# One decoder layer on one core: the two parts of the recurrence's and the branch's weights made by transfers instead of by VectorE

## The chip, the core and the metric

The kernel runs on one core of one Trainium2 chip. A core has a matrix engine (TensorE, PE in the profile; PEld is its loading of stationary operands), VectorE (DVE), ScalarE (ACT), GpSimd (POOL) and SyncE (SP), each with an instruction queue of its own that it executes in order. Transfers between HBM and the on-chip memory SBUF are issued by an engine (here SP or POOL) and then run on 16 DMA engines. Products are accumulated in the banks of PSUM. The metric is the device time of one execution in microseconds, and smaller is better.

## The reference, cut to what matters

One layer for a sequence of 512 tokens with 1024 channels: a SwiGLU feed-forward block, a mixer with two branches (dilated attention, and a gated recurrence), and a second feed-forward block, each between two RMS norms. The part that the change touches:

```python
u = rms_norm(h, mix_norm_pre[l])
proj = u @ w_in[l]                                   # 1024 x 8704
q, k, v, xr, yr, gl = jnp.split(proj, splits, axis=-1)
...
rec = rg_lru_branch(xr, conv_w[l], ...) * jax.nn.gelu(yr)
rec_d = rec @ w_rec_branch[l]                        # 1024 x 1024
gates = jax.nn.sigmoid(gl).reshape(B, S, N_BRANCHES, D_MODEL)
merged = gates[:, :, 0] * attn_d + gates[:, :, 1] * rec_d
h = h + rms_norm(merged @ w_out[l], mix_norm_post[l])
```

`rg_lru_branch` is a causal convolution of width 4, two gates made by small products (`lru_w_x`, `lru_w_a`, 256 x 256 for each of 4 heads) with a sigmoid, and a linear recurrence over the tokens. Everything is float32.

## The kernel before

Channels lie on the 128 partitions and tokens along the free dimension. A product of 1024 by 512 channels and tokens is done in tiles: one weight tile of 128 output channels holds 8 blocks of 128 x 128, for 8 blocks of input channels.

To keep float32 accuracy, each operand is split into a high part in the rounded format fp32r and a low part, also fp32r, that holds the rest. `mm3` (L263 to L266) makes three matmuls of a block: high by high (L264), high weight by low activation (L265), low weight by high activation (L266). `gemm` runs the 8 blocks of a tile, 24 matmuls of 512 columns, into one PSUM bank of tag `acc` (5 banks) or `aux` (3 banks).

All weights stand in one stream in HBM, `wst`, in the order of use (`stream_plan`), and `stream_groups` cuts it into groups of at most 2048 columns, one load each. `raw_of` starts the load of the next group on SP's queue (L199) into one of two buffers of tag `raw`, and hands out its parts. `fetch` takes a tile from there, a buffer of tag `w8` (4 buffers for tiles over 512 columns, each with room for both parts) and makes the parts by `split`:

```python
def split(dh, dl, src):
    ACT.activation(dh, src, AF.Copy)
    DVE.tensor_sub(dl, src, dh.bitcast(F32))
```

L251 is the copy on ACT, which rounds to fp32r; L252 is the subtraction on DVE. In the groups of the profile a weight tile is `w`.

The stages around the change, in the program's order: attention and its branch product (weights ("attn", m), 512 columns, tag `w4`); then the recurrence, a loop over 4 heads; then the branch product with the weights ("rec", m); then `w_out`, and the second feed-forward block. A head of the recurrence does, in this order: two products for `xr` (keys ("in", 36 + c)), each followed by DVE's evacuation (L968), the convolution (ACT L971, DVE L973) and a split into `rec`; two products for `yr` (keys ("in", 44 + c)) with DVE's evacuation (L985) and gelu on ACT (L986); the gates' products from `rec` with the weights ("lru", head), into `aux` banks that ACT's sigmoid empties (L1001); the coefficients and the scan (ACT L1010 to L1017, DVE L1013 to L1022); and a number of products for the branch gate (keys ("in", 60 + c): 0, 2, 2, 4 of them by head) with DVE L1028 and ACT L1029. The branch product has 8 tiles, each followed by DVE (L1036, L1037) and a split. So 24 tiles "in", 4 tiles "lru" and 8 tiles "rec" pass through `w8` there, all of 1024 columns.

The order of the instructions on each engine is not the program's. It is laid out when the kernel is built, by a list scheduler with planned durations: an engine takes the ready instruction with the best priority, and the program's order gives the priority. `tc.high_priority(offset=AHEAD)` lifts the instructions of `fetch` by 100 places, evacuations by 200. Once laid out, each queue is fixed and executes in order; waits are semaphores. POOL's queue before holds only transfers of activations and of the kept residual (L677, L681, L743, L911, L1056, L1067).

Of the kernel before, what the change touches and what calls it, by code (L numbers as in the profile page):

```python
# [10 lines left out]
F32 = mybir.dt.float32  # L11
F32R = mybir.dt.float32r
AF = mybir.ActivationFunctionType
ALU = mybir.AluOpType
AX = mybir.AxisListType

P = 128
# [11 lines left out]
RAW_W = 2048  # L29
# [38 lines left out]
def stream_plan():  # L68

    plan = []  # L70

    def ffn(n):
        for ev in ffn_order():
            if ev[0] == "std":
                plan.append((("gate", n, ev[1]), 1024))
                plan.append((("up", n, ev[1]), 1024))
            elif ev[0] == "prep":
                plan.append((("gu", n, ev[1]), 2048))
            else:
                for m in ev[-1]:  # L80
                    plan.append((("down", n, ev[-2], m), down_width(ev[-2])))
        for m in range(KC):
            plan.append((("down", n, len(FF_PARTS) - 1, m), down_width(len(FF_PARTS) - 1)))

    def values(g):
        for k in range(4):
            plan.append((("v", g, k), 1024))

    def qk(h):
        for g in range(NG):  # L90
            plan.append((("pair", g * 4 + h, 12 + g * 4 + h), 2048))

    ffn(1)
    del plan[:4]
    for k in range(KC):
        plan.insert(k, (("start", k), 512))
    for g in VALUES:
        values(g)
    for h in range(NH):
        qk(h)  # L100
    for c in range(0, KC, 2):
        plan.append((("pair", 52 + c, 53 + c), 2048))
    for m in range(KC):
        plan.append((("attn", m), 512))
    for h in range(NH):
        for c in (2 * h, 2 * h + 1):
            plan.append((("in", 36 + c), 1024))
        for c in (2 * h, 2 * h + 1):
            plan.append((("in", 44 + c), 1024))
        plan.append((("lru", h), 1024))  # L110
        for c in GATE1[h]:
            plan.append((("in", 60 + c), 1024))
    for m in range(KC):
        plan.append((("rec", m), 1024))
    for m in range(KC):
        plan.append((("out", m), 1024))
    ffn(2)
    return plan


def stream_groups():

    groups, cur, w = [], [], 0
    for key, width in stream_plan():
        if w + width > RAW_W or (cur and cur[0][0][0] == "start"):
            groups.append(cur)
            cur, w = [], 0
        cur.append((key, w, width))
        w += width
    groups.append(cur)  # L130
    return groups


SMALL = {}
# [10 lines left out]
def hybrid_layer(ctx: ExitStack, tc: tile.TileContext, xT: bass.AP, wst: bass.AP, small: bass.AP,  # L145
                 consts: bass.AP, bias: bass.AP, out: bass.AP):
    nc = tc.nc
    DVE, ACT, PE = nc.vector, nc.scalar, nc.tensor
# [37 lines left out]


    groups = stream_groups()
    state = {"g": 0, "i": 0, "off": 0, "raw": None}

    def raw_of(key):

        g, i = state["g"], state["i"]
        grp = groups[g]
        if i == 0:
            w = grp[-1][1] + grp[-1][2]
            raw = wpool.tile([P, RAW_W], F32, name="raw", tag="raw", bufs=2)
            src = bass.AP(tensor=wst.tensor, offset=wst.offset + state["off"], ap=[[w, P], [1, w]])
            nc.sync.dma_start(raw[:, :w], src)  # L199
            state["raw"] = raw  # L200
            state["off"] += w * P
        k, o, w = grp[i]
        assert k == key, (k, key)
        src = state["raw"][:, o:o + w]
        if i + 1 == len(grp):
            state["g"], state["i"] = g + 1, 0
        else:
            state["i"] = i + 1
        return src

    def fetch(key, slot=None):

        with tc.high_priority(offset=AHEAD if slot is None else 0):
            src = raw_of(key)
            w = src.shape[-1]
            t = slot() if slot else w8() if w > 512 else w4()
            split(t[:, 0, :w], t[:, 1, :w], src)
            return t[:, 0, :w], t[:, 1, :w]

    def w8():  # L220
        return wpool.tile([P, 2, 1024], F32R, name="w8", tag="w8", bufs=4)

    def w4():
        return wpool.tile([P, 2, 512], F32R, name="w4", tag="w4", bufs=3)
# [25 lines left out]
# [3 lines that stand above are left out]
# [7 lines left out]
    def tmp(name):  # L260
        return tpool.tile([P, T], F32, name=name, tag="t")
# [23 lines left out]
    def gemm_first(keys, x, slots=None):  # L285

        wts = [fetch(k, None if i < 4 else slots.pop(0)) for i, k in enumerate(keys)]
        pss = [acc_ps() for _ in keys]
        for sl in HALVES:
            for k in range(x.n):  # L290
                for wt, ps in zip(wts, pss):
                    mm3(ps[:, sl], k128(wt[0])[:, k, :], k128(wt[1])[:, k, :], x.hi[k][:, sl],
                        x.lo[k][:, sl], k == 0, k == x.n - 1)
        return pss
# [61 lines left out]
    def last_product(key, x, evac, gi, nxt, then, slots, end=False):  # L356
# [6 lines left out]
        for m in range(KC - nl):  # L363
            ps = acc_ps()
            gemm(ps, fetch(key(m)), x)
            evac(m, ps, FULL)
            sq_add(acc, lambda s: facc[:, m, s], FULL, m == 0)
            ACT.activation(facc[:, m, :], facc[:, m, :], AF.Copy, scale=gain(gi, m))
        if nl < 8:
            warm(acc)  # L370
        wts = [fetch(key(m), None if m < 4 else slots.pop(0)) for m in range(KC - nl, KC)]
        for sl in HALVES:
            for m in range(KC - nl, KC):
# [285 lines left out]
    for i, nm in enumerate(("g1b", "g2b")):  # L659
        o, w = SMALL[nm]  # L660
# [25 lines left out]
    with ExitStack() as mx:  # L686
# [59 lines left out]
        t, steps = x_forms("gma", r2, apool, facc)  # L746
# [37 lines left out]
        scale = -1.0 / math.sqrt(P)  # L784
# [117 lines left out]
        for c in range(0, KC, 2):  # L902
            g, u = tmp("g"), tmp("u")
# [17 lines left out]
    with ExitStack() as mx:  # L921
        rpool = mx.enter_context(tc.tile_pool(name="rec", bufs=1))
        rec_t = rpool.tile([P, 16, T], F32R, name="rec")
        rec = Act([rec_t[:, i, :] for i in range(8)], [rec_t[:, 8 + i, :] for i in range(8)])
# [7 lines left out]
        o, w = SMALL["ap"]  # L932
# [26 lines left out]
        for hd in range(NH):  # L959
# [32 lines left out]
            for j in range(2):  # L992
                c = 2 * hd + j
                gs = []
                for w, bn in ((1, "ba"), (0, "bx")):
# [4 lines left out]
                    g = lpool.tile([P, T], F32, name="gt", tag="gt", bufs=4)  # L1000
# [172 lines left out]
```

## Time and profile before

| | |
|---|---|
| median of 3 runs | 1273.09 us (1272.76 to 1273.25) |
| profiled execution, its own time | 1272.06 us |
| its span, first to last instruction | 1270.3 us |
| busy share of the span | PE 98%, PEld 89%, DVE 77%, ACT 56%, POOL 2% |
| recurrence (24 "in" and 4 "lru" tiles) | 649 to 807 us of the span |
| branch product (8 "rec" tiles) | 807 to 851 us |
| HBM read and written | 127.07 MB and 6.29 MB |

How the lines are read: a group of instructions is given as line, engine, operation, output <- input with the count, then the busy time and the mean duration in ns, then the engine's idle time just before these instructions and what ended it. In a row of stages (from:to) the numbers behind the length are the busy time and the count of each engine in the order of its heading, then the granted clock of TensorE, the busy share of the 16 DMA engines and what they moved in GB/s. In a row of waits, "A <- B: us, times, longest" says how long A's engine stood until B was done. A row of transfers gives the count, the size, and the median time from issue to landing.

### The profile page before, as it was taken

The numbers are of one execution on the slowest core, as the hardware profiler recorded it, in microseconds if no ns is written. First come the engines' busy times: TensorE is split into PE (matmuls) and PEld (weight loads), VectorE is DVE, ScalarE is ACT, GpSimd is POOL, SyncE is SP. The second block draws the span as 40 slices with busy tenths as digits, with TensorE's granted clock in tenths as the row PEclk, the third lists the DMA queues.
The fourth block names the chain that finished last, engine by engine and source line by source line (L and its number), as shares of the span: only waits on it lengthen the run. The fifth ranks groups of instructions, "written<-read, shape, count | busy, mean of one in ns | idle before, by whom it ended". The sixth has DMA issues, their size and how long they took to land.

```text
span 1270.3 us, 19619 instructions
## 1 busy us (share of the span) xinstructions
PE 1247.0 (98%) x7952; PEld 1129.1 (89%) x7952; DVE 971.9 (77%) x1561; ACT 715.3 (56%) x1193; POOL 20.0 (2%) x42
## 2 busy tenths in 40 slices
PE   9999999999999999999999999999999999999996
PEld 7889999999887999999988777889988999999995
DVE  7987777777688788889676877753998777777755
ACT  6555444445555565556637997636555544444453
POOL 0000000000002000000100000000000000000000
PEclk9999999999999999999999999999999999999998
DMA  6222222233614322221441231323222222222342
GB/s 238 72 86 102 102 104 104 103 110 113 216 66 148 114 100 83 75 101 68 135 156 41 100 133 67 133 89 111 100 100 91 92 100 100 100 100 86 118 146 67
DMA packets 26937, 135.66 MB, mean 107 GB/s; under 512 B 3424, under 2 KB 5600, under 8 KB 14688
## 3 DMA queue, kind: packets, MB, share of 16 engines
q1 hardware_dynamic: 24192, 122.88, 27.2%
q0 software_dynamic: 2656, 11.54, 2.7%
q8 instruction: 62, 1.02, 0.3%
q14 instruction: 27, 0.22, 0.1%
HBM read 127.07 MB, written 6.29 MB: 105 GB/s over the span
## 4 chain that ended last, share of the span: by engine, by line
PE 69%; DVE 17%; ACT 7%; DMA 4%; issue 2%; SPq 0%; DVEq 0%; ACTq 0%
PE acc L509 10%; PE acc L508 10%; PE acc L510 10%; PE acc L264 9%; PE acc L266 9%; PE acc L265 9%; DVE w L252 4%; DMA raw<-in_w 4%; PE aux L508 2%; PE aux L509 2%; PE aux L510 2%; ACT w L251 2%; DVE sig L973 1%; DVE acc L316 1%; DVE h L436 1%
## 5 line engine op out<-in xcount | busy, mean ns | idle before, releaser
L251 ACT ACTIVATE w<-raw 128x1024 fp32r<-128x1024 f32 (+2 forms) x307 | 263.7, 865 | 231.4 <-PE acc L510 101.2
L252 DVE TENSOR_TENSOR w<-raw,w 128x1024 fp32r<-128x1024 f32 (+2 forms) x307 | 298.6, 986 | 83.8 <-ACT w L251 83.6
L509 PE MATMUL acc<-big,w 128*128 128x256 f32 x928 | 263.3, 284 | 0.0
L508 PE MATMUL acc<-big,w 128*128 128x256 f32 x928 | 263.1, 283 | 0.0
L510 PE MATMUL acc<-big,w 128*128 128x256 f32 x928 | 262.8, 283 | 0.0
L264 PE MATMUL acc<-act,w 128*128 128x512 f32 (+1 forms) x524 | 195.5, 374 | 3.1 <-ACT w L251 2.7
L266 PE MATMUL acc<-act,w 128*128 128x512 f32 (+1 forms) x524 | 191.9, 368 | 1.4 <-DVE w L252 1.2
L265 PE MATMUL acc<-act,w 128*128 128x512 f32 (+1 forms) x524 | 191.6, 366 | 0.0
L508 PEld LDWEIGHTS acc<-big,w 128*128 128x128 f32 x928 | 177.4, 191 | 4.0 <-ACT c L515 0.4
L510 PEld LDWEIGHTS acc<-big,w 128*128 128x128 f32 x928 | 177.7, 191 | 1.8
L509 PEld LDWEIGHTS acc<-big,w 128*128 128x128 f32 x928 | 177.5, 191 | 1.7
L264 PEld LDWEIGHTS acc<-act,w 128*128 128x128 f32 x524 | 98.7, 189 | 20.5 <-ACT w L251 6.0
L266 PEld LDWEIGHTS acc<-act,w 128*128 128x128 f32 x524 | 98.8, 189 | 18.2 <-DVE w L252 4.1
L265 PEld LDWEIGHTS acc<-act,w 128*128 128x128 f32 x524 | 98.9, 189 | 13.7
L515 ACT ACTIVATE c<-acc 128x256 f32<-128x256 f32 x166 | 62.7, 378 | 59.5 <-PE acc L510 57.7
L264 PE MATMUL acc<-big,w 128*128 128x512 f32 (+1 forms) x240 | 91.7, 382 | 0.0
L266 PE MATMUL acc<-big,w 128*128 128x512 f32 (+1 forms) x240 | 91.7, 382 | 0.0
L265 PE MATMUL acc<-big,w 128*128 128x512 f32 (+1 forms) x240 | 91.7, 382 | 0.0
L570 DVE TENSOR_TENSOR facc<-acc,facc 128x512 f32<-128x512 f32 x48 | 33.2, 692 | 57.9 <-PE acc L266 57.7
L509 PE MATMUL aux<-big,w 128*128 128x256 f32 x272 | 76.9, 283 | 0.0
L508 PE MATMUL aux<-big,w 128*128 128x256 f32 x272 | 76.9, 283 | 0.0
L510 PE MATMUL aux<-big,w 128*128 128x256 f32 x272 | 76.8, 282 | 0.0
(273 smaller groups left out, 2455.5 us busy)
## 6 DMA issues: line engine op xcount, KB each, us to landing
raw<-in_w SPq DMA_DIRECT2D x89, 1024.0 KB, 4.9
raw<-in_w SPq DMA_DIRECT2D x23, 512.0 KB, 4.8
raw<-in_w SPq DMA_DIRECT2D x6, 768.0 KB, 4.2
raw<-in_w SPq DMA_DIRECT2D x16, 256.0 KB, 4.4
raw<-in_w SPq DMA_DIRECT2D x3, 896.0 KB, 4.6
h<-in_x SPq DMA_DIRECT2D x8, 256.0 KB, 5.3
h<-in_x POOLq DMA_DIRECT2D x8, 256.0 KB, 5.4
kept_m<-h POOLq DMA_DIRECT2D x2, 1024.0 KB, 4.7
```

Of the source, the lines that this page charges most:

```text
L251: ACT.activation(dh, src, AF.Copy)
L252: DVE.tensor_sub(dl, src, dh.bitcast(F32))
L264: PE.matmul(ps, wh, xh, start=first, stop=False)
L265: PE.matmul(ps, wh, xl, start=False, stop=False)
L266: PE.matmul(ps, wl, xh, start=False, stop=last)
L316: DVE.tensor_add(acc[:, s], acc[:, s], q)
L436: DVE.scalar_tensor_tensor(o, hm(m), col(gname, m), r, op0=ALU.mult, op1=ALU.mult)
L508: PE.matmul(ps, wh, xh, start=start and k == 0, stop=False, skip_group_check=True)
L509: PE.matmul(ps, wh, xl, start=False, stop=False, skip_group_check=True)
L510: PE.matmul(ps, wl, xh, start=False, stop=k == 3, skip_group_check=True)
L515: ACT.activation(c, ps, AF.Copy)
L570: DVE.tensor_add(facc[:, m, :], ps, facc[:, m, :])
```

## The change

For the keys "in" and "rec" (32 tiles) `fetch` no longer goes through a raw buffer. Each such tile is a group of its own in the stream. A casting transfer on POOL's queue brings it from HBM into the high part, rounding on the way; ACT writes the negative of the high part into the low part; a second transfer on POOL's queue brings the same data from HBM again and adds it to the low part. The copy on ACT becomes the negative, and the subtraction on DVE is gone. The tiles "lru" and all others are made as before.

```diff
--- before.py
+++ after.py
@@ -122,13 +122,21 @@
 
     groups, cur, w = [], [], 0
     for key, width in stream_plan():
-        if w + width > RAW_W or (cur and cur[0][0][0] == "start"):
+        if cur and (w + width > RAW_W or cur[0][0][0] == "start" or in_parts(key)):
             groups.append(cur)
             cur, w = [], 0
+        if in_parts(key):
+            groups.append([(key, 0, width)])
+            continue
         cur.append((key, w, width))
         w += width
     groups.append(cur)
     return groups
+
+
+def in_parts(key):
+
+    return key[0] == "rec" or key[0] == "in"
 
 
 SMALL = {}
@@ -211,6 +219,19 @@
     def fetch(key, slot=None):
 
         with tc.high_priority(offset=AHEAD if slot is None else 0):
+            if in_parts(key):
+                grp = groups[state["g"]]
+                w = grp[0][2]
+                assert grp == [(key, 0, w)]
+                src = bass.AP(tensor=wst.tensor, offset=wst.offset + state["off"], ap=[[w, P], [1, w]])
+                state["g"] += 1
+                state["off"] += w * P
+                t = w8()
+
+                nc.gpsimd.dma_start(t[:, 0, :w], src)
+                ACT.activation(t[:, 1, :w], t[:, 0, :w].bitcast(F32), AF.Copy, scale=-1.0)
+                nc.gpsimd.dma_start(t[:, 1, :w], src, accum_op=ALU.add)
+                return t[:, 0, :w], t[:, 1, :w]
             src = raw_of(key)
             w = src.shape[-1]
             t = slot() if slot else w8() if w > 512 else w4()
```

## The prediction

> **What bounds the kernel now.** I read the shares of the engines first, then the slices by stage, then the waits of the stage that the change touches.
>
> ```profile
> span 1270.3 us, 19619 instructions
> PE 1247.0 (98%) x7952; PEld 1129.1 (89%) x7952; DVE 971.9 (77%) x1561; ACT 715.3 (56%) x1193; POOL 20.0 (2%) x42
> ...
> core 0: us, PE busy (x) PEld busy (x) DVE busy (x) ACT busy (x) POOL busy (x), PEclk, DMA share, GB/s
> 649.00:807.00 158.00, 154.18 (x675) 126.01 (x674) 121.12 (x159) 128.15 (x155) 0.00 (x0) 1.00 0.25 91
> 807.00:851.00 44.00, 43.84 (x194) 35.94 (x193) 27.45 (x35) 14.84 (x19) 0.00 (x0) 1.00 0.32 118
> ```
>
> PE is busy for 98% of the span. The change lies in two stages: the recurrence (649 to 807 us) and the product with the branch weights (807 to 851 us). PE idles there for 158.00 - 154.18 = 3.8 us and 44.00 - 43.84 = 0.2 us. All that the change can win in its own stages is therefore some 4 us. DVE is busy for 77% and ACT for 81% of the recurrence; POOL has no instruction in either stage. The granted clock is 1.00, so the clock explains nothing here.
>
> What PE waited for in the window of 640 to 810 us, from the table of waits:
>
> ```profile
> engine line waited for: us in total, times, longest us
> PE aux L264 <- ACT gt L1001: 2.2, 2, 1.8
> PE aux L265 <- DVE rec L252: 1.0, 1, 1.0
> PE aux L266 <- DVE w L252: 0.6, 1, 0.6
> ```
>
> Of the 3.8 us, ACT's sigmoids of the gates hold 2.2 and DVE 1.0 + 0.6 = 1.6. Next is the pace that the weights must keep. These are the matmuls of the second stage, from the view of the tile rec (first and last start are the last two numbers before the form), and the weights' own instructions in the recurrence, from the groups by form:
>
> ```profile
> L264 PE MATMUL acc<-rec,w x64: 387/389/396, 807.4 to 850.7; 128*128 128x512 f32 x64
> ...
> L251 ACT ACTIVATE w<-raw 128x1024 fp32r<-128x1024 f32 x29 | 30.3, 1052 | 18.7 <-DMA raw<-in_w 9.5 <-PE acc L266 9.2
> ...
> L252 DVE TENSOR_TENSOR w<-raw,w 128x1024 fp32r<-128x1024 f32 x29 | 34.9, 1215 | 3.7 <-ACT w L251 3.6
> ```
>
> 64 of the first of three matmuls start within 43.3 us: 63 steps of 0.687, so a weight tile (8 steps) is used up in 5.5 us. The tag w8 has 4 buffers. A buffer that comes free at the end of one product is needed again three products later: the refill has 3 x 5.5 = 16.5 us. Today the raw data lies ready in SBUF and the refill is 1.05 us on ACT and 1.2 us on DVE. The cover is large, which is why PE waits only 0.6 us for a lo part.
>
> **The change part by part.**
>
> Removed, DVE: 32 subtractions (24 keys "in", 8 keys "rec"), 32 x 1.215 = 38.9 us. DVE is not the bound. On the path lie only the two waits above, at most 1.6 us; I take -1.6 because DVE at 77% falls to (121.12 - 24 x 1.215) / 158 = 58%. The ends are 0 (another instruction of DVE holds PE instead) and -3.8 (the sigmoids come earlier as well).
>
> Exchanged, ACT: 32 negatives for 32 copies of the same shape, 1.05 us each: 0 in busy time. What differs is what stands ahead of them, below.
>
> Removed, SP: the loads of these 32 tiles, 512 KB each. The landing times of all loads:
>
> ```profile
> raw<-in_w SPq DMA_DIRECT2D x89, 1024.0 KB, 4.9
> raw<-in_w SPq DMA_DIRECT2D x23, 512.0 KB, 4.8
> ...
> h<-in_x POOLq DMA_DIRECT2D x8, 256.0 KB, 5.4
> kept_m<-h POOLq DMA_DIRECT2D x2, 1024.0 KB, 4.7
> ...
> kept<-h POOLq DMA_DIRECT2D x2, 1024.0 KB, 4.2
> ```
>
> SP's loads ran ahead through two raw buffers of 1 MB, so they cost PE nothing; the four lru tiles stay there, each now a load of its own, as do the w_out tiles, which can only come earlier. I take 0 for SP.
>
> Added, DMA: 64 transfers of 512 KB in place of 32.
>
> ```profile
> DMA packets 3052, 22.31 MB, mean 101 GB/s; under 512 B 336, under 2 KB 336, under 8 KB 336
> ## 3 DMA queue, kind: packets, MB, share of 16 engines
> q1 hardware_dynamic: 3041, 22.16, 27.8%
> ```
>
> That is 640 to 860 us: 22.16 MB took 27.8% of 220 us, so 0.524 MB takes 1.45 us of all 16 engines. The casting transfer takes 1.45 if casting is free. The adding one reads its source and its destination: between 1.45 and 2 x 1.45 = 2.9. At most 4.4 us in each 5.5: the engines suffice unless casting or adding is itself slow, which no row shows. The Trainium skill, "Collectives: The Full Stack", on reduce-scatter, says that the slower step there is not the add but its second source read; by that the 2.9 would be the price. No run here shows an adding transfer.
>
> Added, POOL: 64 issues. The issues that the trace has, in order of time:
>
> ```profile
> 315.31 3.85 POOL L677 DMA_DIRECT2D h<-in_x  x7 [314.87 <-PE acc L510]
> 320.81 0.55 POOL L677 DMA_DIRECT2D h<-in_x  x1 [1.65 <-issue]
> 373.43 0.54 POOL L681 DMA_DIRECT2D kept_m<-h  x1 [52.08 <-DVE h L354]
> ```
>
> An issue is 0.54 us; 64 make 35 us on an engine that is idle. (Seven in a row go out without a gap, the eighth 1.65 us late; with two or three in flight I take 0, at worst 1.65 now and then.)
>
> Added, three waits in a row. The casting transfer waits for its w8 buffer; the negative waits for the cast to land; the adding transfer waits for the negative. By itself the chain fits: 4.8 (the 512 KB row) + 1.05 + adding 4.8 (if like a load) to 9.6 (if it takes twice as long) = 10.7 to 15.5 of 16.5 us. So a buffer refilled at once is ready in time, with 1 to 6 us for delays where there were 14.
>
> But POOL executes in order, and both transfers of all tiles are in its one queue. What stands behind a waiting adding transfer is the next tile's cast. If the queue runs cast, add, cast, add, the next cast is issued only when the former has landed, ACT has negated and the add is issued: 4.8 + 1.05 + 0.54 = 6.4 us a tile, plus ACT's delay before the negative. Ends of the 6.4: 4.2 for the landing (the fastest row of POOL) gives 5.8, 5.4 (the slowest) gives 7.0. ACT's delay lies between 0 (it stands idle, waiting) and 1.84 (three sigmoids in a row, the row below, which a negative can meet); with ACT 81% busy I take 0.5. That makes 6.9 us a tile against 5.5 that PE needs, 5.5 x 28 / 24 = 6.4 on average over the recurrence, where four lru tiles by the old path stand between.
>
> ```profile
> 783.39 1.84 ACT L1001 ACTIVATE gt<-aux,sm 128x512 f32<-128x512 f32 x3
> ```
>
> In the same way the negative, waiting, holds what is behind it on ACT: the sigmoids that free the aux banks and give the gates, the conv's first tap, the gelu. PE waits for the first of these already (2.2 us). ACT idles for 158 - 128.15 = 29.9 us, or 1.2 us for each of 24 negatives: waits up to that are covered, longer ones lengthen the stage.
>
> Whether cast or add comes first in POOL's queue is decided when the queues are laid out: the add is first if its negative was planned to end within one product (5.5 us) of the former cast. By the rows, 4.8 + 1.05 = 5.9 is just above that. But the plan is earlier than the chip where a landing is concerned: ACT's weight copies, put where the plan had them ready, waited for loads for 9.5 us in the recurrence (the L251 row above). So I take the serial order as the likelier.
>
> The sum. Four tiles are in their buffers when the recurrence begins; 24 - 4 + 8 = 28 refills follow, the first when the first product has ended, at 649.5 + 5.5 = 655. Their chain ends at 655 + 28 x 6.9 = 848.2, and the last add lands 4.8 to 9.6 later: 853 to 858, middle 855.4. PE would begin the last product at 851 - 5.5 = 845.5. So the last product is 9.9 us late; less 1.6 from DVE: +8.3. What follows (w_out and the second FFN) keeps its time. The profiled execution took 1272.06 us, 1.0 below the median of 1273.09; 1272.06 + 8.3 = 1280.4, and on the median 1281.4. I predict 1281.
>
> The ends: with a delay of 0 on ACT and a landing of 4.2, 655 + 28 x 5.8 + 7.2 = 824.6, and nothing is late at all; with 1.0 on ACT, 28 x 7.4 + 655 + 7.2 = 869.4, 23.9 late, so 1273.1 + 23.9 - 1.6 = 1295.
>
> **The rivals.**
>
> 1. Hidden: not slower. POOL's queue has the next cast ahead of the former add, or the cast lands within 5.5 - 1.05 - 0.54 = 3.9 us. Then each refill ends within 15.5 of its 16.5 us and only DVE's 1.6 us remain: 1271.5. For it: 5.9 against 5.5 is close, and a few places of the other order restore the lead. Against it: no 512 KB load has a median below 4.8. The Trainium skill, "DMA: Bandwidth & Descriptors", Anatomy of one DMA, gives 2.0 us and the bytes over 436 GB/s for a transfer issued by GpSimd. For 512 KB that is an estimate of 3.2 us, which would put the whole chain at 4.8 us a tile and this rival first. The trace's POOL rows, 4.2 to 5.4 us, do not agree with 3.2, though the 4.2 is for twice the bytes.
>
> 2. The transfers themselves are slow. If adding lands after 15 us, a buffer's turn is 4.8 + 1.05 + 0.54 + 15 + 5.5 = 26.9 us, a quarter of it 6.7 a tile whatever the order: 28 x (6.7 - 5.5) = 34 us, so 1307. It decides from an adding time of 16.5 - 6.4 = 10.1 us on. For it: nothing measured says that an adding or casting transfer runs at a copy's rate. Against it: the engines are 70% idle in these stages.
>
> 3. Faster. With a quarter less work in the recurrence DVE gives xr, the conv and the scan earlier, ACT's waits for it end, and the sigmoids hold PE no more: all 3.8 us go, 1269.3. For it: ACT's queue is the cause of PE's largest wait. Against it: the negatives now wait for a landing on that same queue.
>
> **How the numbers follow.** From an unchanged kernel a measurement of this one can tell a difference of about 0.2%, 2.5 us. Serial queue 0.42 (of it 0.06 so mild that it is within 2.5 us), hidden 0.36 (0.06 of it by more than 2.5 us faster), slow transfers 0.14, faster 0.08. Faster: 0.06 + 0.08 = 0.14; same: 0.06 + 0.30 = 0.36; slower: 0.36 + 0.14 = 0.50. The range goes from 1270.5, below the hidden case, to 1301, above the serial case's upper end of 1295; it leaves out most of rival 3 and the worse half of rival 2. The serial case's own range is 1273 to 1295.
>
> **What would show it.** On POOL in 649 to 851 us: cast and add in turn, each add waiting for ACT, each cast behind it; PE waiting for DMA at L266 (the lo part) and L264, most in the second stage. If hidden: two casts side by side, PE's waits at 4 us or less, ACT waiting for DMA under 30 us. If transfers are slow: landings of the add above 10 us. DVE must lose 39 us of busy time in any case. I am wrong if PE's idle time grows outside of these stages, if ACT's table loads (their order may change) are the new limit, or if a DMA in flight delays SP's loads for the stages behind.

## The result and the profile after

The changed kernel is slower: a median of 1294.37 us (1290.15 to 1296.13, 4 runs) against 1273.03 us (1272.76 to 1273.25, 4 runs), a ratio of 1.0163 with a 95% interval of 1.0147 to 1.0179. The prediction was 1281 us, with a range of 1270.5 to 1301.0. The direction held, the time lies in the range, and the mechanism is the one forecast; the loss of 21 us is two and a half times the 8 us that were forecast.

The heading of the page after, and its slices of the two stages (the branch product begins at 820 us instead of 807):

```profile
span 1288.4 us, 19699 instructions
PE 1251.2 (97%) x7952; PEld 1131.2 (88%) x7952; DVE 937.0 (73%) x1529; ACT 703.0 (55%) x1184; POOL 65.9 (5%) x106
...
core 0: us, PE busy (x) PEld busy (x) DVE busy (x) ACT busy (x) POOL busy (x), PEclk, DMA share, GB/s
649.00:820.00 171.00, 157.35 (x676) 128.45 (x675) 96.16 (x135) 114.16 (x143) 31.13 (x44) 0.98 0.63 150
820.00:869.00 49.00, 45.22 (x196) 36.14 (x195) 20.30 (x29) 15.09 (x20) 9.02 (x13) 1.00 0.69 167
```

The span grew by 1288.4 - 1270.3 = 18.1 us, and the two stages by 220 - 202 = 18: all of it is here. PE idles for 13.65 + 3.78 = 17.4 us in them, where it was 4.0; the other 4.6 us are busy time of PE, most of it matmuls at a lower clock (last section). DVE's busy time fell by 34.9 us over the span. ACT lost 12 us as well, though its negatives cost what the copies did: in the recurrence it now loads its function tables 24 times and not 33, and its instructions stand in another order.

What PE waited for (620 to 880 us), and what ACT and POOL waited for:

```profile
PE aux L285 <- ACT gt L1022: 13.6, 4, 4.8
PE acc L287 <- DMA w<-in_w: 3.6, 3, 2.3
...
ACT w L232 <- DMA w<-in_w: 48.9, 14, 7.7
...
POOL w L233 <- ACT w L232: 139.4, 30, 9.5
POOL w L231 <- PE acc L287: 38.2, 9, 21.0
POOL w L231 <- PE aux L287: 9.6, 3, 4.0
```

L231 is the cast, L232 the negative, L233 the add. POOL stood 139.4 us at adds whose negative was not made, and only 47.8 (38.2 + 9.6) at casts whose buffer was not free. But PE's own largest wait names ACT's sigmoids, not a transfer: by this view alone, ACT's queue could be the cause, held for 48.9 us by negatives that wait for a cast to land. The queue of POOL, in order of time, with what each instruction waited for:

```profile
639.63 0.86 POOL L233 DMA_DIRECT2D w<-in_w  x1 [1.85 <-ACT w L232]
661.50 0.55 POOL L231 DMA_DIRECT2D w<-in_w  x1 [21.02 <-PE acc L287]
666.92 0.86 POOL L233 DMA_DIRECT2D w<-in_w  x1 [4.86 <-ACT w L232]
667.55 0.79 POOL L231 DMA_DIRECT2D w<-in_w  x1
676.37 0.86 POOL L233 DMA_DIRECT2D w<-in_w  x1 [8.03 <-ACT w L232]
676.95 0.84 POOL L231 DMA_DIRECT2D w<-in_w  x1
...
847.31 0.88 POOL L233 DMA_DIRECT2D w<-in_w  x1 [6.28 <-ACT w L232]
848.80 0.86 POOL L233 DMA_DIRECT2D w<-in_w  x1 [0.60 <-ACT w L232]
849.35 0.88 POOL L231 DMA_DIRECT2D w<-in_w  x1
858.25 0.86 POOL L233 DMA_DIRECT2D w<-in_w  x1 [8.02 <-ACT w L232]
```

A cast that stands right behind an add (667.55, 676.95, 849.35) had no wait of its own: its buffer was free already, and it waited only for its turn. 14 of the 28 casts from 661.50 us on stand so, 2 more right behind another cast, and 12 waited for their buffer. From the first refill at 661.50 to the last at 849.35 it is 187.85 / 27 = 6.96 us from cast to cast.

### The profile page after: what moved, and what is told of

Its sections match the earlier page's. It is cut to its first block, busy times and chain, and to the rows that moved or that the text cites. A ratio compares the mean times of both kernels' runs of the same rounds, so it can differ in the third digit from the quotient of the medians.

```text
span 1288.4 us, 19699 instructions
## 1 busy us (share of the span) xinstructions
PE 1251.2 (97%) x7952; PEld 1131.2 (88%) x7952; DVE 937.0 (73%) x1529; ACT 703.0 (55%) x1184; POOL 65.9 (5%) x106
## 3 DMA queue, kind: packets, MB, share of 16 engines
q0 software_dynamic: 11872, 45.10, 13.9%
## 4 chain that ended last, share of the span: by engine, by line
PE 68%; DVE 12%; issue 9%; DMA 5%; ACT 4%; POOL 2%; DVEq 0%; SPq 0%; POOLq 0%; ACTq 0%
PE acc L529 9%; PE acc L530 9%; PE acc L531 9%; PE acc L285 9%; PE acc L287 9%; PE acc L286 8%; DVE w L273 3%; DMA w<-in_w 3%; DMA raw<-in_w 3%; PE aux L531 2%; PE aux L529 2%; PE aux L530 2%; ACT w L272 1%; DVE h L457 1%; POOL w L233 1%
## 5 line engine op out<-in xcount | busy, mean ns | idle before, releaser
L272 ACT ACTIVATE w<-raw 128x512 fp32r<-128x512 f32 (+2 forms) x275 | 230.3, 844 | 202.6 <-PE acc L531 97.9
L273 DVE TENSOR_TENSOR w<-raw,w 128x512 fp32r<-128x512 f32 (+2 forms) x275 | 260.5, 961 | 87.0 <-ACT w L272 86.9
L287 PEld LDWEIGHTS acc<-act,w 128*128 128x128 f32 x524 | 98.8, 189 | 18.4 <-DVE w L273 4.2
```

What stands on the lines that cost most here:

```text
L287: PE.matmul(ps, wl, xh, start=False, stop=last)
```

## The experiments

Three theories remained. A: ACT's in-order queue, where the negatives that wait for a landing hold the sigmoids. B: POOL's in-order queue, where casts stand behind adds. C: the transfers are slow by themselves. A fourth, D, is in one expectation: four buffers are too few. Ratios are to the kernel before, on the same chip.

**The negative on DVE.**

```diff
-ACT.activation(t[:, 1, :w], t[:, 0, :w].bitcast(F32), AF.Copy, scale=-1.0)
+DVE.tensor_scalar(t[:, 1, :w], t[:, 0, :w].bitcast(F32), -1.0, None, op0=ALU.mult)
```

> The changed kernel with the negative made by DVE instead of ACT; all else, both transfers and their order on POOL, by the same rules. Theory A (ACT's in-order queue: the negatives that wait for the cast to land hold the sigmoids behind them, and PE waits for those): PE's wait for the gates' sigmoids falls from 13.6 us to about the 2.2 of before, and the time to 1274 to 1283. Theory B (POOL's in-order queue: casts stand behind adds that wait for negatives): the chain of cast, negative, add is as long as it was, time 1290 to 1296. Theory C (the transfers are slow by themselves): 1290 to 1296 too, with PE waiting for DMA.

Measured: 1298.8 us, ratio 1.0197 (1.0182 to 1.0213), slower still than the changed kernel and above all three expectations. PE's and POOL's waits, and DVE's:

```profile
PE acc L287 <- DMA w<-in_w: 8.8, 7, 2.4
PE aux L287 <- DVE w L273: 4.6, 1, 4.6
PE aux L285 <- ACT gt L1022: 3.3, 2, 2.9
...
DVE w L232 <- DMA w<-in_w: 69.7, 14, 8.6
...
POOL w L233 <- DVE w L232: 136.3, 23, 8.4
```

The sigmoids are all but cleared (3.3 us), as A says, and the time is no better: now DVE is held, and PE waits for the add itself. POOL's wait, 136.3 us, is about the same. So the sigmoids were where the lateness showed, and clearing them does not save the time. That a waiting negative does the harm on whichever engine makes it, this run cannot exclude; the two orders of POOL's queue and the rec tiles, below, do.

**Without the add.**

```diff
-nc.gpsimd.dma_start(t[:, 1, :w], src, accum_op=ALU.add)
```

> The changed kernel without its adding transfers (the low part is left as the negative of the high part, so part of the weights' value is left out). Theory A: ACT's negatives still wait for casts to land, now without the adds ahead of the casts; the wait of ACT for DMA falls from 49 us by less than half, time 1280 to 1290. Theory B: nothing is ahead of a cast but the buffer, time 1270 to 1276. Theory C (adding is slow): PE's waits for DMA go, 3.6 us, but not those for the sigmoids: 1287 to 1292.

Measured: 1272.65 us, ratio 0.9996 (0.9984 to 1.0007): all of the loss is gone. ACT's negatives still wait for casts for 26.9 us, against 48.9 in the changed kernel, the fall by less than half that A named; but the time is B's. PE waits 3.6 us in all, no more than before the change:

```profile
PE aux L284 <- ACT gt L1021: 3.6, 2, 2.2
...
ACT w L232 <- DMA w<-in_w: 26.9, 15, 3.5
...
w<-in_w POOLq DMA_DIRECT2D x32, 512.0 KB, 3.9
```

A cast alone on the queue lands in 3.9 us, faster than SP's plain load of that size (4.8): casting is not slow. This speaks for B but does not exclude a slow add, since the add is gone with its place in the queue.

**POOL's order, next cast first.** The add is issued behind the cast of the next tile (shortened; the last tile before an lru tile has no next one, and its add follows its own cast):

```diff
-nc.gpsimd.dma_start(t[:, 0, :w], src)
-ACT.activation(t[:, 1, :w], t[:, 0, :w].bitcast(F32), AF.Copy, scale=-1.0)
-nc.gpsimd.dma_start(t[:, 1, :w], src, accum_op=ALU.add)
+nxt = cast() if in_parts(groups[state["g"]][0][0]) else None   # buffer and cast of the next tile
+ACT.activation(t[:, 1, :w], t[:, 0, :w].bitcast(F32), AF.Copy, scale=-1.0)
+with tc.issue_after(nxt[3].ins):                               # order on POOL's queue only
+    nc.gpsimd.dma_start(t[:, 1, :w], src, accum_op=ALU.add)
```

> The changed kernel with POOL's order written out: each add is issued behind the cast of the next tile of its kind, so that no cast in the chain stands behind the add just before it (cast, add of the tile before, cast, add of the tile before, and so on); within a head only, since the lru tile ends the chain. Theory A: the casts come earlier by a few us at most, the negatives still wait at the head of ACT's queue: 1284 to 1294. Theory B: 1271 to 1280, POOL's waits for the negative fall well below the 139 us of the changed kernel.

Measured: 1275.32 us, ratio 1.0016 (1.0006 to 1.0025). Instructions, bytes and buffers are the same, and of the changed kernel's 1.63% loss 0.16% are left. POOL's queue and the waits:

```profile
809.81 0.55 POOL L227 DMA_DIRECT2D w<-in_w  x1 [3.81 <-PE acc L295]
812.05 0.88 POOL L239 DMA_DIRECT2D w<-in_w  x1 [1.70 <-ACT w L235]
815.25 0.55 POOL L227 DMA_DIRECT2D w<-in_w  x1 [2.31 <-PE acc L295]
816.08 0.87 POOL L239 DMA_DIRECT2D w<-in_w  x1 [0.29 <-issue]
820.69 0.55 POOL L227 DMA_DIRECT2D w<-in_w  x1 [3.73 <-PE acc L295]
...
PE aux L293 <- ACT gt L1030: 3.9, 2, 2.9
...
POOL w L239 <- ACT w L235: 28.6, 17, 4.7
POOL w L241 <- ACT w L235: 19.5, 5, 7.0
...
ACT w L235 <- DMA w<-in_w: 28.6, 12, 4.2
```

L239 and L241 are the adds; POOL's waits for negatives fell from 139.4 to 28.6 + 19.5 = 48.1 us, as B says. Each cast (L227) now waits for its buffer alone and goes out the moment a product ends, in the branch product every 5.44 us, which is PE's own pace. The cast still has to land before the negative, ACT still waits 28.6 us for that, the add still takes its time: all of it fits under three products, as the prediction's 10.7 to 15.5 of 16.5 us said. B is shown. C falls with it: the 27 adds of L239 land in 6.9 us (median) against 5.5 in the changed kernel, the casts in 4.9 against 6.1. A pair takes 11.8 us in sum against 11.6, and nine tenths of the loss are gone.

**POOL's order, strictly cast, add.** Each add joins the list `adds`, and each cast is issued behind the last of them (shortened):

```diff
-nc.gpsimd.dma_start(t[:, 0, :w], src)
+with tc.issue_after(adds[-1].ins) if adds else ExitStack():    # the add of the tile before
+    nc.gpsimd.dma_start(t[:, 0, :w], src)
```

> The changed kernel with POOL's order written out the other way: each cast is issued behind the add of the tile before, through all 32 tiles. Theory B (a tile costs cast, negative and add one after the other wherever the cast stands behind the add): the step becomes 6.1 for the cast's landing in the changed kernel, 1.06 for the negative, 0.87 for the add's issue, 8.0 us in all; 28 refills from 661.5 end at 886, the add lands 5.5 later, against 863.9 in the changed kernel: 27 us more, so 1315 to 1325. Theory A (ACT's queue): the negatives wait no longer than now, 1290 to 1300.

Measured: 1333.97 us, ratio 1.0478 (1.0460 to 1.0495). The direction is that of B, the size is above the 1315 to 1325 expected. The end of its queue:

```profile
884.61 0.88 POOL L236 DMA_DIRECT2D w<-in_w  x1 [7.01 <-ACT w L235]
885.20 0.84 POOL L234 DMA_DIRECT2D w<-in_w  x1
893.29 0.87 POOL L236 DMA_DIRECT2D w<-in_w  x1 [7.25 <-ACT w L235]
893.87 0.86 POOL L234 DMA_DIRECT2D w<-in_w  x1
901.83 0.87 POOL L236 DMA_DIRECT2D w<-in_w  x1 [7.10 <-ACT w L235]
```

From the first refill at 664.67 to 893.87, 27 steps of 8.49 us: a cast's landing (median 6.4), the negative 1.06, the add's issue until the next cast 0.59, and a rest of 0.4, which would be ACT's delay. The expectation had 8.0, most of the difference being the landing, 6.1 there. The chain also began 3 us later. So the changed kernel's 6.96 is a mixture: its queue often has two casts side by side, which the strict order never has.

**A buffer of their own for the lru tiles.** The first line keeps the priority that these tiles had:

```diff
-with tc.high_priority(offset=AHEAD if slot is None else 0):
+with tc.high_priority(offset=AHEAD if slot is None or key[0] == "lru" else 0):
...
-wh, wl = fetch(("lru", hd))
+wh, wl = fetch(("lru", hd), lambda: rpool.tile([P, 2, 1024], F32R, name="wx", tag="wx", bufs=1))
```

> The changed kernel with a buffer of its own for the four lru tiles, so that the casts need not stand back for them: the first refill of the chain can begin when the first product of the recurrence ends (655) and not the second (661.5). Theory B with a rate of 7 us a tile: the chain begins 6.5 us earlier and keeps its rate: 1285 to 1290. Theory D (four buffers are too few for the latency, whatever the order): all of the loss beyond 4 us goes, 1273 to 1279.

Measured: 1289.72 us, ratio 1.0127 (1.0112 to 1.0142), 4.7 us less than the changed kernel and at the upper end of what B expected. The first refill is issued at 656.50 instead of 661.50; the last cast at 842.4, so a step is 6.88 us against 6.96, and POOL still waits 123.9 us for negatives in the whole run. More room moves the start of the chain and hardly its rate. D falls, with the kernel that lost next to nothing with the same four buffers.

**The change for the rec tiles alone.**

```diff
-return key[0] == "rec" or key[0] == "in"
+return key[0] == "rec"
```

> The change for the eight rec tiles alone; the in tiles as before. Theory B: eight refills at 7 us, where PE takes 5.4, lose 8 x 1.6 = 12.8 us, of which the cover of one refill (16.3 less a chain of about 12.5) takes back 3.8: 9 us, 1280 to 1284; less where POOL's order has two casts side by side. Theory A: ACT has little else to do in this stage (14.8 of 44 us), so nothing is held: 1272 to 1275.

Measured: 1280.73 us, ratio 1.0061 (1.0046 to 1.0077), 7 us lost in a stage where ACT was busy for a third of the time before. That is the lower end of B's numbers and outside of A's: PE waited 4.5 us for adds, and 1.6 for sigmoids, no more than the 2.2 of before.

**The cast alone, on the kernel before.** The low part is subtracted by DVE from the raw data, as before (shortened):

```diff
-split(t[:, 0, :w], t[:, 1, :w], src)
+nc.gpsimd.dma_start(t[:, 0, :w], src_in_hbm)
+DVE.tensor_sub(t[:, 1, :w], src, t[:, 0, :w].bitcast(F32))
```

> One part of the change alone, on the kernel before: the high part of the in and rec tiles by the casting transfer from POOL's queue, the low part as before by DVE's subtraction from the raw buffer; no negative and no add, and ACT's copies of these tiles are gone. Theory A: ACT has no wait for the cast and 33 us less work, so the sigmoids come in time: 1268 to 1273, unless DVE's subtraction, which now waits for the landing, holds DVE's queue in the same way (then 1275 to 1285). Theory B: no add and so no chain: 1269 to 1274. Theory C (casting is slow by itself): over 1280, with PE waiting for DMA.

Measured: 1279.0 us, ratio 1.0045 (1.0030 to 1.0059), where B expected no loss, and within the 1275 to 1285 that A gave for DVE being held. No chain is left on POOL, but DVE's subtractions now wait for the landing and hold DVE:

```profile
DVE w L225 <- DMA w<-in_w: 32.5, 9, 6.8
...
ACT rec L261 <- DVE sig L983: 22.4, 7, 4.0
...
PE aux L274 <- ACT gt L1011: 5.5, 3, 3.5
```

The part of A that may stand: a wait for a landing at the head of a compute queue can cost on its own account. The waits above lead from the landing by DVE and ACT to PE, and 5 us were lost; no run tried this link by itself. ACT bore 27 to 29 us of such waits next to without loss in the kernel without adds and in the one with the next cast first.

## Why the prediction was right in kind and wrong in size

**Right.** That PE has 4 us to win at most and DVE's 39 us are worth next to nothing (the kernel without adds has them off DVE as well, at a ratio of 0.9996); that the chain fits by itself; and that POOL's in-order queue makes it a serial one where the add was put ahead of the next cast, which is so for 14 of the 28.

**Right by luck.** The rate, 6.9 us a tile against 6.96 between casts. The 6.9 was for a queue strictly in turn, and written out so it measured 8.49: a cast lands in 6.4 us there, not in 4.8. In the changed kernel (6.1) the casts side by side take much of this back. The two errors cancel.

**The end of the chain** was the term that failed, and with it the credit for DVE below. The last add was to land at 855.4 us. The chain that ended last shows when it did, and that the last product waited for it:

```profile
858.25 5.63 DMA w<-in_w
...
863.93 0.50 PE acc L287
```

The add issued at 858.25 landed at 863.9, 8.5 later than the sum had it. By parts:

- The start, +6.5 us. I had the first refill begin when the first product ends (655). The first buffer that comes free does not go to a cast: head 0 has four in tiles, then the lru tile. Its copy on ACT waited for exactly that buffer, and the first cast got the next one, at 661.50 in the queue above.

```profile
655.69 1.06 ACT L272 ACTIVATE w<-raw 128x1024 fp32r<-128x1024 f32 x1 [12.97 <-PE acc L287]
```

I had counted the lru tiles' time on PE but not their place among the buffers. The kernel with a buffer of their own got 5.0 us of this start and 4.7 us of the time back.

- The steps, +4.4: from 661.50 to the end of the last add's issue, 859.1, 28 steps of 7.06, against 6.9.
- The last landing, -2.4: 4.8 after the issue's end, not 7.2, the middle of 4.8 to 9.6.

The sum is 6.5 + 4.4 - 2.4 = 8.5.

**The credit of 1.6 us for DVE** was not paid. PE's waits for DVE went, but PE's waits for the sigmoids and then for the adds were there instead, and the time of the last product was set by the last add: less work on DVE could not move it. With 9.9 + 8.5 = 18.4 us of lateness and no credit, the span's 18.1 is accounted for to within 0.3.

**The rest.** The profiled execution took 1290.15 us, the lowest of the four; the median is 4.2 higher, where the sum took the 1.0 of the kernel before. The others had spans of 1292.3, 1292.9 and 1294.4 at mean granted clocks of 0.993, 0.989 and 0.988, against 1288.4 at 0.994 for the profiled one. The two with the lowest clock are the longest, but the first of them is 3.9 us longer at nearly the same clock. What makes these 3 us stays open.

**The rivals.** Hidden became true as soon as the order of the queue was turned, at 1275 us and not 1271.5. For the casts, the runs measured 3.9 us alone, and beside adds 6.1 in the changed kernel and 4.9 with the next cast first. The fit in the Trainium skill, "DMA: Bandwidth & Descriptors", Anatomy of one DMA, gives an estimate of 3.2 us for 512 KB; the measurement decides. Slow transfers as the cause were excluded. Of the signs named, the pairs of cast and add on POOL and the 39 us off DVE (38.1 of its subtractions, 34.9 in all) were there. PE's waits were not mostly at L266's successor and not mostly in the second stage: lateness reached PE by way of ACT first.

## What to carry to other kernels

When a step is moved to transfers, write down the queue that issues them, in order, and look for an instruction that waits for another engine ahead of one that is ready: there the latency of each item adds up instead of overlapping. If both orders keep the data right, fix the one that issues the next independent transfer before the dependent one; here that alone was worth 19 us of 21. And count who takes the next free buffer, all users of the tag, before dating the first refill.

## What the runs showed of the hardware

The adding transfer is dearer than the casting one, on the engines and at issue. From the queues of three kernels, GpSimd's software queue:

```profile
q0 software_dynamic: 2656, 11.54, 2.7%
```

```profile
q0 software_dynamic: 7264, 28.32, 6.9%
```

```profile
q0 software_dynamic: 11872, 45.10, 13.9%
```

These are the kernel before, the one without adds, and the changed one. 6.9% of 1273.3 less 2.7% of 1270.3 is 53.6 us for 32 casts, 1.67 each; 13.9% of 1288.4 less 87.9 is 91.2 us for 32 adds, 2.85 each, if the casts cost there what they cost without adds: 1.7 times as much as a cast for the same bytes. The prediction's bound was 2.9, twice a plain load's 1.45. The Trainium skill, "Collectives: The Full Stack", on reduce-scatter, says that the second source read makes that step slower and not the add itself; the 2.85 agrees with it. An add's issue on POOL takes 0.87 us, where a cast without one ahead of it takes 0.55. The adds of the changed kernel, from the view of their line:

```profile
L233 POOL DMA_DIRECT2D w<-in_w x32: 856/874/904, 626.4 to 858.3; - x32
...
DMA to landing us min/median/max: 5.1/5.5/10.0
```

After two waits of PE for a sigmoid, of 4.3 us (until 710.7) and 4.8 us (until 755.3), the granted clock was below full, and matmuls began 0.43 us apart where 0.23 is usual. The second of them, in its slice of 10 us and in the chain that ended last:

```profile
750.00:760.00 10.00, 5.20 (x17) 3.81 (x16) 0.69 (x1) 5.37 (x8) 1.99 (x3) 0.83 0.56 141
...
754.53 0.70 ACT gt L1022
755.27 0.75 PE aux L285
756.03 0.43 PE aux L286
756.45 0.43 PE aux L287
```

The clock, 0.83 over the slice, is 0.50 from 756 to 758 us, and likewise from 712 to 714. After waits of 2.5, 2.4 and 2.1 us (until 678.5, 852.6 and 797.3) it stayed at 1.00. Each of the two long waits so cost 1.7 us more than its length: after the second, eight matmuls took 3.5 us from start to start, where the usual pace gives 1.8. That is 3.4 of the 4.6 us by which PE's busy time grew in the two stages; the rest was not traced.
